# Feed-forward down steps spread over the last pairs, condition rows loaded earlier, and the final norm's first half given precedence

## The chip, the cores and the metric

The kernel runs on one core of one Trainium2 chip. The metric is the device time of one execution in microseconds (us), here the median of three runs. The engines are named as in the profile: PE is TensorE (PEld its weight loads), DVE is VectorE, ACT is ScalarE, POOL is GpSimd, SP is SyncE, whose queue issues most of the loads.

## What is computed

Two layers of a diffusion backbone work on 512 latent tokens and 256 context tokens of 1024 channels. Each layer is a half-step feed-forward, token mixing, and another half-step feed-forward; the output is the final RMSNorm of the latent tokens. Cut to what matters here:

```python
def half_ffn(x, shift, scale, gate, g, w_gate, w_up, w_down):
    h = rmsnorm(x, g) * (1 + scale) + shift
    return x + 0.5 * gate * swiglu(h, w_gate, w_up, w_down)   # silu(h @ w_gate) * (h @ w_up) @ w_down

mod_l = (silu(c) @ ada_w[layer] + ada_b[layer])               # nine shift, scale and gate vectors
...
return rmsnorm(x_l, final_g)
```

The hidden width of the feed-forward is 2816, which is 22 blocks of 128. The four feed-forwards are called f0 and f1 (layer 0) and f2 and f3 (layer 1). f3 computes latent tokens only, since the context isn't needed after it.

## The kernel before, in words

Activations lie with channels on partitions. Every fp32 matrix product is three matmuls on operands split in a rounded high part and a rest (`mm3`, lines 296 to 299): a weight tile of 128x512 is loaded by SP (`wraw`, L132), cast by ACT to its high part (L120) and subtracted by DVE to its low part (L121); that is `wsplit`. There are six raw slots (`w32p`) and eight slots each of high and low parts (`wp`).

A feed-forward (`ffn`) runs over eleven pairs of hidden blocks. The first pair is computed plainly (`Pair`). Each pair j from 1 to 10 builds two matrices (`Mat`), gate and up, each as seven block products of half the tokens (numbers 1 to 7, L478), from sums and differences of weight blocks that POOL forms (L453, L454, L465, L467). A product is twelve matmuls of 384 columns (256 in f3). Between products, ACT copies and DVE combines partial sums (L483, L496), applies the SiLU (L502), multiplies gate and up (L510) and splits the result into the activations `ah` and `al`. The products of one pair are issued as gate 1, the former pair's up 4, gate 5, 2, 6, 3, 7, up 1, gate 4, up 5, 2, 6, 3, 7, so there are 14 to a pair.

The down projection of a finished pair is a generator of eight steps (`dsteps`), one for each block of 128 output channels. A step (`down`, L312) multiplies the two hidden blocks of the pair with their weights into a PSUM tile `sm`, of which there are three, and DVE adds it to the residual stream x with the gate as factor (L323). Before the first and the fifth step, two down weight tiles are loaded and split. When a pair j up to 9 has issued its gate product 5, the eight steps of pair j-1 join a queue, and after every product `dstep` (L533) takes one step from it (two in f0's pair 2). So the steps come between the first eight products after that point, the other six have none, and pair 10 has none. The down projection of the last two pairs (blocks 18 to 21) follows after the loop, first for part of the tokens, then for the others: latent and then context tokens in f0 and f2, two halves of 384 tokens in f1, two halves of 256 latent tokens in f3.

Beside the products, `Background` computes the modulation vectors that later stages need, on DVE. Its condition rows (`scb`, 128x1024) come in two halves: load (L204), Silu on ACT (L205), then for each of its vectors eight steps, each of a 256 KB load (L211) and one or two DVE reductions (L215), which are pinned behind the DVE work traced before them. `tick`, called after each product, takes steps at `rate` per product. There is one slot for the condition rows, so the second half's load waits for the last reduction of the first half. In the neighbourhood mixer the same class loads through POOL's queue. In f3 it has no vectors to compute, and only loads and activates the rows.

`final` (L1102) norms the latent tokens in two halves of 256: squares on ACT, additions on POOL and for the last two on DVE (L254, L255), column sums and a broadcast by matmuls with ones (L259, L274), with twelve small DVE operations between (`st`, L262 to L269) and a scaled diagonal (L272), then eight multiplies on DVE (L1111) into a ring of four tiles, each sent out by SP (L1113).

Order: the program order is a priority. A planner walks the instructions when the kernel is built and puts on each engine the earliest in program order among those that it takes to be ready; a block under `high_priority(offset=400)` counts as 400 instructions earlier. On the chip each engine keeps the order so found.

## Time and profile before

| | us |
|---|---|
| median of three runs | 2666.29 |
| lowest and highest | 2664.46, 2667.95 |
| the profiled execution | 2665.89 |
| its span, first to last instruction | 2664.1 |
| PE busy | 2537.8 (95%) |
| DVE busy | 2127.7 (80%) |
| ACT busy | 1189.4 (45%) |
| POOL busy | 641.6 (24%) |

The mean granted clock of TensorE was 0.979 of its full 2.4 GHz. All times below are microseconds from the start of the profiled span. f0 takes the time to about 595, f1 that from about 950 to 1470, f2 from there to about 1985, f3 from about 2260 to the final norm at 2647. The view of waits tells for each engine whom it waited for; the timeline gives each instruction with its start, its duration and, in brackets, how long its engine stood idle before it and what ended that; the table of stretches gives each engine's busy time in a stretch and the mean granted clock.

### The profile page before, as it was taken

To read this page: it belongs to the slowest core of one execution; us is meant where nothing else is said; L and a number is where in the kernel's file an instruction comes from. 1 tells how busy PE (TensorE), PEld (TensorE's weight loads), DVE (VectorE), ACT (ScalarE), POOL (GpSimd) and SP (SyncE) were. 2 spreads that over 40 slices of the span, in tenths; PEclk is the share of its full clock that TensorE was granted. 3 is DMA by queue.
4 is the path that set the end of the run, shared out by engine and by line. 5 is a ranking of instruction groups with operands and counts; after the bars stand their busy time and mean duration, and the time that the engine had idled before them with its cause. 6 is when DMAs were issued, how large, how long until landed. Compare 5 with 4: busy or idle time off the path is not lost. (4 is left out here: it accounts for less than half of the span.)

```text
span 2664.1 us, 41381 instructions
## 1 busy us (share of the span) xinstructions
PE 2537.8 (95%) x14860; PEld 2321.8 (87%) x14860; DVE 2127.7 (80%) x4316; ACT 1189.4 (45%) x2435; POOL 641.6 (24%) x513
## 2 busy tenths in 40 slices
PE   6999999999999899999999999999999998899997
PEld 4889989987898799999999999999986787899987
DVE  8878888888578687787778879789788775888876
ACT  6533333344238663334334533343335554644443
POOL 2321322221210142132222422222201100433331
PEclk8999999999999899999999999999999999999998
DMA  6334333343465022333332224344432110233332
GB/s 232 96 98 121 102 108 108 104 127 115 147 179 133 15 80 84 107 95 100 99 95 72 83 88 151 119 131 134 124 111 64 49 32 1 83 104 98 97 100 67
DMA packets 145357, 269.92 MB, mean 101 GB/s; under 512 B 17664, under 2 KB 23808, under 8 KB 145152
## 3 DMA queue, kind: packets, MB, share of 16 engines
q1 hardware_dynamic: 139360, 250.82, 30.7%
q0 software_dynamic: 4640, 15.73, 1.8%
q8 instruction: 116, 1.90, 0.3%
q10 hardware_dynamic: 1152, 0.74, 0.1%
q14 instruction: 89, 0.73, 0.1%
HBM read 258.84 MB, written 8.39 MB: 100 GB/s over the span
## 5 line engine op out<-in xcount | busy, mean ns | idle before, releaser
L120 ACT CAST whi<-w 128x512 fp32r<-128x512 f32 (+2 forms) x826 | 500.1, 617 | 777.6 <-PE bg L298 358.2
L121 DVE TENSOR_TENSOR wlo<-w,whi 128x512 fp32r<-128x512 f32 (+2 forms) x826 | 633.5, 785 | 161.7 <-ACT whi L120 153.6
L297 PE MATMUL sm<-ah,whi 128*128 128x512 f32 (+2 forms) x1488 | 512.5, 345 | 11.7 <-DVE x L323 9.8
L298 PE MATMUL sm<-al,whi 128*128 128x512 f32 (+2 forms) x1488 | 511.9, 344 | 0.0
L299 PE MATMUL sm<-ah,wlo 128*128 128x512 f32 (+2 forms) x1488 | 509.8, 343 | 0.0
L323 DVE SCALAR_TENSOR_TENSOR x<-sm,mod,x 128x512 f32<-128x512 f32 (+3 forms) x712 | 421.4, 613 | 56.6 <-PE sm L299 52.3
L297 PEld LDWEIGHTS sm<-ah,whi 128*128 128x128 f32 x1488 | 282.0, 190 | 47.5 <-DVE x L323 15.0
L299 PEld LDWEIGHTS sm<-ah,wlo 128*128 128x128 f32 x1488 | 282.0, 190 | 31.9 <-issue 0.5
L298 PEld LDWEIGHTS sm<-al,whi 128*128 128x128 f32 x1488 | 283.6, 191 | 27.4 <-DVE al L121 0.5
L453 POOL TENSOR_TENSOR s<-w,w 128x512 f32<-128x512 f32 x80 | 106.9, 1337 | 809.7 <-DMA w<-in_ffn_gu 716.4
L467 POOL TENSOR_TENSOR w<-w,w 128x512 f32<-128x512 f32 x80 | 122.4, 1530 | 389.9 <-DVE wlo L121 200.4
L255 POOL TENSOR_TENSOR acc<-acc,sq 128x384 f32<-128x384 f32 (+1 forms) x50 | 46.4, 928 | 427.6 <-ACT sq L254 426.6
L120 ACT CAST whi<-s 128x512 fp32r<-128x512 f32 x80 | 49.7, 621 | 222.1 <-POOL s L453 75.4
L496 DVE TENSOR_TENSOR c<-bg,c 128x384 f32<-128x384 f32 (+1 forms) x160 | 83.4, 521 | 67.0 <-PE bg L299 65.5
L297 PE MATMUL bg<-B11h,whi 128*128 128x384 f32 (+1 forms) x384 | 128.1, 334 | 8.4 <-ACT B11h L120 5.8
L299 PE MATMUL bg<-B11h,wlo 128*128 128x384 f32 (+1 forms) x384 | 128.6, 337 | 5.3 <-DVE wlo L121 5.3
L120 ACT CAST ah<-c 128x384 fp32r<-128x384 f32 (+1 forms) x176 | 85.1, 486 | 103.2 <-DVE c L510 91.4
L298 PE MATMUL bg<-B11l,whi 128*128 128x384 f32 (+1 forms) x384 | 128.2, 334 | 0.0
L465 POOL TENSOR_TENSOR w<-s,w 128x512 f32<-128x512 f32 x80 | 120.1, 1501 | 10.7 <-DVE wlo L121 3.7
L297 PE MATMUL bg<-B22h,whi 128*128 128x384 f32 (+1 forms) x352 | 118.4, 336 | 1.8 <-ACT c L483 1.6
L454 POOL TENSOR_TENSOR w<-w,w 128x512 f32<-128x512 f32 x80 | 116.0, 1449 | 6.3
L297 PE MATMUL bg<-T3h,whi 128*128 128x384 f32 (+1 forms) x320 | 107.5, 336 | 8.6 <-DVE c L496 8.6
(384 smaller groups left out, 6648.0 us busy)
## 6 DMA issues: line engine op xcount, KB each, us to landing
w<-in_ffn_gu SPq DMA_DIRECT2D x352, 256.0 KB, 2.8
gt<-in_ada_t SPq DMA_DIRECT2D x208, 256.0 KB, 2.7
w<-in_ffn_d SPq DMA_DIRECT2D x176, 256.0 KB, 2.9
w<-in_ada_w SPq DMA_DIRECT2D x48, 256.0 KB, 4.6
gt<-in_ada_t POOLq DMA_DIRECT2D x32, 256.0 KB, 3.2
w<-in_ab_in SPq DMA_DIRECT2D x24, 256.0 KB, 2.7
scb<-in_cond_rows SPq DMA_DIRECT2D x8, 512.0 KB, 4.5
w<-in_ab_out SPq DMA_DIRECT2D x16, 256.0 KB, 3.8
```

What stands on the lines that cost most here:

```text
L120: nc.scalar.copy(hi, src)
L121: (eng or nc.vector).tensor_tensor(lo, src, hi.bitcast(F32), op=ALU.subtract)
L255: (nc.vector if i >= len(srcs) - 2 else adder).tensor_tensor(acc[:, :n], acc[:, :n], sq[:, :n], op=ALU.add)
L297: nc.tensor.matmul(out, whi, xhi, start=first, stop=False, skip_group_check=more)
L298: nc.tensor.matmul(out, whi, xlo, start=False, stop=False, skip_group_check=more)
L299: nc.tensor.matmul(out, wlo, xhi, start=False, stop=last, skip_group_check=more)
L323: nc.vector.scalar_tensor_tensor(o, p[:, a - t0:a - t0 + m], gate[:, d, v:v + 1], o, op0=ALU.mult, op1=ALU.add)
L453: nc.gpsimd.tensor_tensor(s1, a21, a22, op=ALU.add)
L454: nc.gpsimd.tensor_tensor(a21, self.src[1], a21, op=ALU.subtract)
L465: nc.gpsimd.tensor_tensor(self.src[6], self.src[5], self.src[6], op=ALU.subtract)
L467: nc.gpsimd.tensor_tensor(self.src[3], self.src[3], self.src[6], op=ALU.subtract)
L496: nc.vector.tensor_tensor(self.c[p], ps, self.c[p], op=ALU.add)
```

## The change

Three things change. `dstep` now adds a fraction to an account after every product and takes a step whenever the account reaches one: 8/14 a product up to pair 8, 8/20 in pairs 9 and 10, two in f0's pair 2 as before. What the queue still holds after the loop is issued there. `Background` yields twice between the load of the second half of the condition rows and its Silu, and twice more before the first reduction that uses it; its rate counts these four. `final` puts all that it does for each half under `high_priority(offset=400)`, adds the squares on DVE instead of POOL, and has eight output tiles.

```diff
-            self.rate = 2 * KD * len(mods) / steps
+            self.rate = (2 * KD * len(mods) + 4) / steps
...
                 self.queue.dma_start(scb, A["cond_rows"][:, :, hs])
+                if half:
+                    yield
+                    yield
                 nc.scalar.activation(scb, scb, AF.Silu)
+                if half:
+                    yield
+                    yield
...
-                    dstep(2 if first and self.j == 2 else 1)
+                    dstep(2.0 if first and self.j == 2 else 8.0 / 14.0 if self.j < np2 - 2 else 8.0 / 20.0)
...
+            paid = [0.0]
+
             def dstep(n):
-                for _ in range(n):
+                paid[0] = min(paid[0] + n, 2.0) if queue else 0.0
+                while paid[0] >= 1.0 - 1e-6:
+                    paid[0] -= 1.0
                     while queue and next(queue[0], 0) == 0:
                         queue.pop(0)
...
                 prev = u
+            while queue:
+                dstep(1.0)
             later.finish()
...
-            fp = pool("fp", 4, st)
+            fp = pool("fp", 8, st)
             for (t0, n, v) in HALVES:
                 sl = slice(t0, t0 + n)
-                pb = rms_rows([xk[k][:, sl] for k in range(KD)], n, D, np_, nc.gpsimd, "sm" if t0 else "nr")
-                for k in range(KD):
-                    o = fp.tile([P, 512], F32, name="o")
-                    nc.vector.scalar_tensor_tensor(o[:, :n], xk[k][:, sl], fg[:, k:k + 1], pb[:, :n],
-                                                   op0=ALU.mult, op1=ALU.mult)
-                    nc.sync.dma_start(A["out"][k][:, sl], o[:, :n])
+                with tc.high_priority(offset=400):
+                    pb = rms_rows([xk[k][:, sl] for k in range(KD)], n, D, np_, None, "sm" if t0 else "nr")
+                    for k in range(KD):
+                        o = fp.tile([P, 512], F32, name="o")
+                        nc.vector.scalar_tensor_tensor(o[:, :n], xk[k][:, sl], fg[:, k:k + 1], pb[:, :n],
+                                                       op0=ALU.mult, op1=ALU.mult)
+                        nc.sync.dma_start(A["out"][k][:, sl], o[:, :n])
```

## Rows read from the trace of the kernel before

**Rows 1.** Busy time, share of the span and instructions of each engine.

```profile
PE 2537.8 (95%) x14860; PEld 2321.8 (87%) x14860; DVE 2127.7 (80%) x4316; ACT 1189.4 (45%) x2435; POOL 641.6 (24%) x513
```

**Rows 2.** Stretches: length, busy us of each engine (instructions), PEclk, DMA share, GB/s.

```profile
482.00:529.00 47.00, 47.00 (x268) 44.10 (x268) 41.12 (x77) 16.97 (x32) 11.23 (x8) 1.00 0.34 107
529.00:561.00 32.00, 29.64 (x166) 28.11 (x165) 29.08 (x56) 13.85 (x27) 7.62 (x5) 1.00 0.44 134
1390.00:1422.00 32.00, 28.24 (x157) 26.58 (x156) 27.54 (x50) 13.21 (x26) 7.39 (x5) 1.00 0.42 129
1918.00:1950.00 32.00, 29.85 (x165) 27.84 (x164) 26.55 (x51) 14.22 (x28) 7.37 (x5) 1.00 0.44 129
2562.00:2592.00 30.00, 30.00 (x205) 27.61 (x206) 22.36 (x38) 14.22 (x30) 11.57 (x8) 1.00 0.34 106
2592.00:2620.00 28.00, 24.30 (x183) 23.23 (x181) 20.33 (x31) 13.41 (x31) 7.23 (x5) 0.94 0.31 95
382.00:389.00 7.00, 6.77 (x23) 6.20 (x24) 5.00 (x10) 1.55 (x3) 0.74 (x1) 0.55 0.22 71
2606.00:2611.00 5.00, 5.00 (x32) 5.00 (x32) 2.77 (x4) 1.48 (x4) 1.29 (x1) 0.66 0.35 92
```

**Rows 3.** Timeline of PE, last pairs: first and last two of nine waits.

```profile
543.74 0.44 PE L297 MATMUL bg<-T2h,whi 128*128 128x384 f32 x1 [1.57 <-ACT c L483]
...
2604.48 0.38 PE L297 MATMUL bg<-B11h,whi 128*128 128x256 f32 x1 [1.60 <-DVE c L510]
2605.71 0.39 PE L297 MATMUL bg<-T2h,whi 128*128 128x256 f32 x1 [0.85 <-ACT c L483]
```

**Rows 4.** Timeline of ACT in f0: the Silu of the second condition rows.

```profile
373.91 1.06 ACT L205 ACTIVATE scb<-scb 128x1024 f32<-128x1024 f32 x1 [2.33 <-DMA scb<-in_cond_rows]
```

**Rows 5.** Timeline of DVE behind it.

```profile
375.01 0.75 DVE L215 CUSTOM_DVE_ANT_0 go<-gt,scb,mod 128x512 bf16<-128x512 f32 x1 [1.70 <-ACT scb L205]
...
375.80 1.66 DVE L215 CUSTOM_DVE_ANT_0 gt<-gt,scb,mod 128x512 f32<-128x512 f32 x1
...
381.43 1.13 DVE L323 SCALAR_TENSOR_TENSOR x<-sm,mod,x 128x512 f32<-128x512 f32 x2
```

**Rows 6.** Timeline of PE behind that.

```profile
382.23 0.79 PE L297 MATMUL sm<-ah,whi 128*128 128x512 f32 x1 [3.16 <-DVE x L323]
```

**Rows 7.** Timeline of DVE in the tail.

```profile
2647.03 0.48 DVE L323 SCALAR_TENSOR_TENSOR x<-sm,mod,x 128x256 f32<-128x256 f32 x1
...
2649.18 0.16 DVE L262 TENSOR_SCALAR st<-sm 128x2 f32<-128x2 f32 x1 [0.43 <-PE sm L259]
...
2651.61 0.16 DVE L269 SCALAR_TENSOR_TENSOR st<-st 128x2 f32<-128x2 f32 x1
2652.38 1.66 DVE L1111 SCALAR_TENSOR_TENSOR o<-x,c_final_g,nr 128x256 f32<-128x256 f32 x4 [0.61 <-PE nr L274]
...
2659.41 1.93 DVE L1111 SCALAR_TENSOR_TENSOR o<-x,c_final_g,sm 128x256 f32<-128x256 f32 x4 [0.42 <-DMA out<-o]
```

**Rows 8.** Timeline of PE in the tail: the first half's broadcast.

```profile
2651.26 1.08 PE L274 MATMUL nr<-dg,ones 128*128 128x256 f32 x2 [2.12 <-DVE st L269]
```

**Rows 9.** Timeline of PE: one down step and the product after it.

```profile
495.37 0.39 PE L297 MATMUL sm<-ah,whi 128*128 128x512 f32 x1
...
496.77 0.28 PE L297 MATMUL sm<-ah,whi 128*128 128x256 f32 x1
...
497.49 0.34 PE L297 MATMUL bg<-T2h,whi 128*128 128x384 f32 x1
```

**Rows 10.** Groups by line, whole span: busy us, mean ns, idle before them.

```profile
L121 DVE TENSOR_TENSOR wlo<-w,whi 128x512 fp32r<-128x512 f32 (+2 forms) x826 | 633.5, 785 | 161.7 <-ACT whi L120 153.6
```

**Rows 11.** Groups by line in the tail, 2628 to the end.

```profile
L255 POOL TENSOR_TENSOR acc<-acc,sq 128x256 f32<-128x256 f32 x10 | 7.4, 736 | 31.1 <-ACT sq L254 30.8
...
L255 DVE TENSOR_TENSOR acc<-acc,sq 128x256 f32<-128x256 f32 x4 | 1.7, 426 | 1.0 <-ACT sq L254 0.6 <-POOL acc L255 0.2
```

**Rows 12.** Waits by engine: who waited for whom, us, times, longest.

```profile
ACT whi L120 <- PE bg L298: 397.1, 264, 5.1
```

## The prediction

> **What bounds the kernel now.** I read the engine totals first: PE is busy 95% of the span, DVE 80%, ACT 45% [rows 1]. So time can only come out where PE waits or runs at half clock, and the next view is the table of stretches [rows 2]. In a steady pair of the first feed-forward (482 to 529) PE is busy all 47.0 us and DVE 41.1 of them; in f3's (2562 to 2592) PE has 30.0 of 30 us. In the last pair of each feed-forward PE is short: 29.6 of 32, 28.2 of 32, 29.9 of 32 and 24.3 of 28 us. There the kernel issues 14 products and no down step, so PE consumes weights fastest just where POOL, ACT and DVE must make them at the same rate as before. The PE timeline names the waits [rows 3]: in the last pairs PE stands idle nine times, 11.5 us in all: 2.36 in f0 (two), 3.46 in f1 (two), 1.97 in f2 (two), 3.71 in f3 (three); the rows show the first and the last two of the nine. Each ends on a combination or copy by DVE or ACT of the product before, which was itself late. After f3's spell the granted clock averages 0.66 over 2606 to 2611 [rows 2], half speed for part of it, which costs another 5 x 0.34 = 1.7 us. Pool of the first edit: 13.2 us.
>
> The second place is in the middle of f0. At 373.91 ACT starts the Silu on the second half of the condition rows after 2.33 us of idling for their DMA [rows 4]; DVE's reduction behind it starts 1.70 us late, and the following one takes 1.66 us instead of 0.75 [rows 5]. The x updates of the down steps come only at 381.43, their PSUM tiles are not freed, and PE idles 3.16 us until 382.23 [rows 6]. Then the granted clock averages 0.55 over 382 to 389 [rows 2], which loses 7 x 0.45 = 3.1 us. Pool: 6.3 us.
>
> The third is the tail. The last x update starts at 2647.03 [rows 7] and the last output multiply ends at 2661.34. Between lies the final norm of both halves: the broadcast matmuls of the first half run only at 2651.26 [rows 8], behind the last down matmul in PE's order, the four-deep output ring makes DVE wait for outgoing DMAs three times (0.42 us at the last, [rows 7]), and the second half's multiplies queue behind the first's.
>
> **Part 1, down steps spread.** Nothing is added or removed. A step is six matmuls of 512 columns and, where context tokens are computed, six of 256: 2.12 us of PE from 495.37 to 497.49, 1.40 of it for the latent tokens alone, which is f3's step [rows 9]. On DVE it is two x updates, 1.13 us for the 512 and the 256 together [rows 5]. Every fourth step issues two weight loads on SP, two ACT casts and two DVE subtractions of 0.79 us mean [rows 10]. Counting the new rates over the 14 products of a pair, steady pairs keep eight steps, now between all products instead of the first eight; pair 9 gets six, and pair 10 four, after product 5 and 6 of gate and 1 and 5 of up. The second weight half of that group thus moves on SP, ACT and DVE past the loads and splits of pair 10's first products. In steady pairs I cost the move at nothing: what hides it is a PE stream without gaps, where the part of a pair without down steps is already full [rows 2]; if that cover goes, see the rival on slots.
>
> In pair 10 four steps give PE 4 x 2.12 = 8.5 us (f3: 5.6) that doesn't need new product weights, and DVE 4 x 1.13 = 4.5 us (f3, taking two thirds: 3.0) plus two subtractions, 1.6 us, that can delay the chain. Net cover is 8.5 - 4.5 - 1.6 = 2.4 us in f0 to f2 and 5.6 - 3.0 - 1.6 = 1.0 in f3; without the subtractions, which needn't lie on the chain, 4.0 and 2.6. Against the idle time above this gives 2.36 + 2.4 + 1.97 + 1.0 = 7.7 us, or 2.36 + 3.46 + 1.97 + 2.6 = 10.4. I take the middle, 9.1; bounds 4.9 (rival 1) and 13.2 (the pool).
>
> The Trainium skill (Perfetto Trace Analysis, Identifying the Most-Contended Engine) says that matmul busy time is a poor measure of headroom, and to use the weight loads' busy share. By that, with 44.1 of 47 us as full [rows 2], the four last pairs lack 2.0, 3.7, 2.3 and (27.6 of 30 as full) 2.5 us, 10.5 together instead of 13.2, and the sum would fall by 2.7 x 9.1/13.2 = 1.9 us. I keep the idle rows, which name their waits.
>
> **Part 2, condition rows.** Per second half: DMA as before, two background steps, Silu, two steps, first reduction. The pace of steps rises by 4/64 to 4/48, so reductions come a little earlier and the total is the same. The DMA keeps its place on SP (POOL in the mixer) behind the last reduction that reads the old rows, so what queues behind it there still waits. What goes is ACT's 2.33 us in front of weight casts and DVE's 1.70 us, and for four steps no reduction asks DVE for time. Next late would be POOL's weight sums that slow DVE from 375.8 on, which happen with every matrix and don't stop PE elsewhere. I take 5.0 of 6.3; low bound 0, if that slowing alone caused the stall. The other nine Silus cost PE nothing now: no spell of PE idling follows them. In f3, whose background has no modulation, the two loads and Silus (1.06 us each, [rows 4]) are issued in the loop instead of at its end; ACT is busy 14.2 of 30 us there [rows 2], so nothing.
>
> **Part 3, final norm.** In the order now, the second half's chain alone would be: first small operation at 2649.18 [rows 7], its twelve operations by 2651.61 at the latest, which is when the last of both chains starts, two diagonal scalings 0.5, broadcast matmuls 1.1 [rows 8], eight multiplies at 0.41 to 0.48 (1.66 and 1.93 for four, in both rows): 2649.2 + 2.4 + 0.5 + 1.1 + 3.5 = 2656.7 against 2661.3, a gain of 4.6. Against it, the first half's column sums and broadcast (0.5 and 1.08 us of PE) now stand inside the last down products, where PE has no gap: 1.6 back. The additions leave POOL (0.736 us) for DVE (0.426) [rows 11]: ten more on DVE, 4.3 us, beside x updates of 0.48 per 0.72 and then 1.44 us of PE time, and the first half's multiplies come on top; DVE is nearly full there, so up to 1.5 us can come back too, or none. I take 3.0, bounds 1.5 and 4.6.
>
> **Sum.** 9.1 + 5.0 + 3.0 = 17.1 us. The profiled execution took 2665.9 us (span 2664.1 and 1.8 around it), 0.4 under the median of the runs: 2666.3 - 17.1 = 2649.2.
>
> **Rivals.** (1) DVE sets the pace of the last pairs. It is busy 29.1, 27.5, 26.6 of 32 and 20.3 of 28 us [rows 2]. If that share is all it can give, adding 6.1 us of DVE work (f3: 4.6) stretches the pairs to 38.7, 39.1, 39.3 and 34.3 us, where PE alone needs 38.1, 36.7, 38.4 and 29.9: 8.3 of 13.2 stays lost, part 1 gives 4.9, the time is 2666.3 - 4.9 - 5.0 - 3.0 = 2653.4. For it: operations of DVE that take twice their time while POOL works, as the 1.66 us [rows 5]. The Trainium skill (SBUF — State Buffer, SBUF: two separate sides) states that of a DVE instruction with two SBUF inputs and a GpSimd instruction that reads SBUF, the one that starts second waits for the whole of the other; by that rule this rival is right. Against it: DVE reached 41.1 of 47 us in the steady pair with POOL at work and PE never waited. Chance 0.18.
> (2) The planner, not the program's order, decides. It issues what is ready, so the four steps may be used as filling in pair 9, where product 1 of the next matrix is used now, and the final's first half may stay behind; parts 1 and 3 fall away, part 2 stays: 2666.3 - 5.0 = 2661.3. Against: the steps' own weights come later in program order now, so they can't be ready as early. Chance 0.13.
> (3) Slower: a down step's split weights occupy two of the eight slots for seven products instead of four. ACT already waits 397 us for PE to release a slot, 264 times [rows 12]. If product weights then come late once per steady pair (27 pairs in the four loops) by 1.57 us, as at 543.74 [rows 3], that is 42 us: 2666.3 - 17.1 + 42 = 2691. It decides from 17.1/27 = 0.63 us per pair upwards. Against: each step's weights are as many as before, and an even use of PE asks for a product weight every 3.3 us instead of 2.1 in the part without down steps. Chance 0.10.
>
> **How the numbers follow.** The forecast has 0.59: 2649, its own range 2642 (the pools, 13.2 + 6.3 + 4.6 = 24.1) to 2657 (4.9, 3.0 and 1.5 for the three parts). The range takes in rival 1 and most of 2, and 3 us below the pools for single PE waits that the loops hold besides the nine: 2639 to 2663. About 0.2%, 5.3 us, is what a measurement of this kernel can tell from no change, so faster means under 2661.0: forecast and rival 1, 0.77; within 0.2%: rival 2, 0.13; slower: rival 3, 0.10.
>
> **What would show it.** Part 1: in the last pairs four groups of down matmuls (sm from ah) between products 5 and the up matrix's 2, PE idle below 4 us over the four, and no drop of the clock at f3's end; rival 1 would show the idle still there under DVE releasers. Part 2: no ACT idle for the condition rows' DMA, and no 3 us PE spell in f0's middle. Part 3: the first half's broadcast before the last down matmul, no DVE wait on outgoing DMAs, and about 10 us from the last x update to the last multiply. Rival 3 would show as PE waiting in steady pairs on whi or wlo. The forecast is wrong if the steady pairs lose what they now have, a PE without gaps.

## The result, and the profile after

The changed kernel took 2705.74 us (median of four runs, 2703.23 to 2707.99) against 2665.38 for the kernel before on the same chip: ratio 1.015, 95% interval 1.0133 to 1.0167. It is 40 us slower, where 17 us less was forecast. (Every ratio below is to the kernel before, run on the same chip.) Its profiled execution has a span of 2702.5 us. The engine totals of its page differ little from before: PE has the same 2538 us of work, DVE 27 us more [rows 1].

```profile
PE 2538.0 (94%) x14860; PEld 2320.3 (86%) x14860; DVE 2154.4 (80%) x4326; ACT 1191.4 (44%) x2435; POOL 641.8 (24%) x503
```

So the time went into waits of PE. To find the stage, I cut each span at the starts of the column-sum matmuls of the norms, which every kernel has in the same places. The rows of PE's timeline below are the cuts at the beginning of f2, of m1 (the second mixer), of f3 and of the tail.

```profile
1474.26 0.80 PE L265 MATMUL sm<-ones,acc 128*128 128x1 f32 x6 [1.72 <-DVE acc L261]
...
2018.56 0.50 PE L265 MATMUL sm<-ones,acc 128*128 128x1 f32 x4
...
2298.23 0.60 PE L265 MATMUL sm<-ones,acc 128*128 128x1 f32 x4 [1.87 <-DVE acc L261]
...
2691.03 0.61 PE L265 MATMUL sm<-ones,acc 128*128 128x1 f32 x4 [1.54 <-DVE acc L261]
```

f2 took 2018.56 - 1474.26 = 544.3 us, f3 2691.03 - 2298.23 = 392.8. The table gives all stages in this way, for every kernel that ran; m0 and m1 are the mixing stages between the feed-forwards. The medians are of all runs of a kernel (two to eleven), the stages of its one profiled execution.

| kernel | median us | f0 | m0 | f1 | f2 | m1 | f3 | tail |
|---|---|---|---|---|---|---|---|---|
| before | 2666.3 | 595.7 | 344.1 | 529.3 | 530.9 | 278.9 | 369.7 | 15.6 |
| after | 2705.7 | 595.3 | 347.1 | 531.9 | 544.3 | 279.7 | 392.8 | 11.5 |
| e1_spread | 2717.2 | 595.7 | 352.3 | 537.9 | 542.7 | 279.2 | 393.6 | 15.7 |
| e2_rest | 2665.7 | 593.3 | 347.5 | 526.2 | 534.3 | 278.0 | 372.9 | 11.5 |
| e3_late | 2667.5 | 594.6 | 348.8 | 527.6 | 531.2 | 276.7 | 370.3 | 11.5 |
| e4_copy | 2699.5 | 600.4 | 349.8 | 532.5 | 547.6 | 276.0 | 380.9 | 11.5 |
| e5_raw | 2708.9 | 597.1 | 348.8 | 532.4 | 544.0 | 279.9 | 393.8 | 11.5 |
| e6_slots | 2692.9 | 597.0 | 349.7 | 532.4 | 545.2 | 278.7 | 376.5 | 11.5 |
| e7_thin | 2677.7 | 597.4 | 346.3 | 532.5 | 544.3 | 275.8 | 361.9 | 11.5 |
| e8_fill | 2698.4 | 598.1 | 350.5 | 532.4 | 546.0 | 277.5 | 383.1 | 11.5 |
| e9_norm | 2662.0 | 591.0 | 345.7 | 528.8 | 530.9 | 276.4 | 371.5 | 11.5 |
| e10_f0rows | 2662.9 | 592.4 | 345.8 | 528.4 | 531.2 | 278.4 | 373.5 | 11.5 |
| e11_few | 2678.7 | 594.0 | 351.6 | 529.0 | 530.7 | 276.3 | 385.0 | 15.7 |
| e12_both | 2677.0 | 597.1 | 350.2 | 532.4 | 543.0 | 277.3 | 363.0 | 11.5 |
| e13_f2fill | 2695.9 | 597.9 | 344.1 | 532.0 | 534.5 | 278.6 | 392.5 | 11.4 |
| e14_f2thin | 2691.3 | 600.1 | 346.3 | 531.6 | 525.8 | 277.3 | 398.6 | 11.5 |

Stages from different executions differ by some us without any cause in the program: e9_norm has before's order of instructions in f0, and its f0 is 4.7 us shorter; e11_few has before's order up to f3, and its m0 is 7.5 us longer. So what stands out for the changed kernel is f3 (+23.1), f2 (+13.4) and the tail (-4.1). In the kernels with the new pace whose edit leaves f2 as it is, f2 takes 542.7 to 547.6 us, and f3, where it is left as it is, 392.5 to 398.6: what an experiment does to f2 or f3 is to be seen against these.

The table of stretches of the changed kernel (columns as in [rows 2]) shows where in a feed-forward it happens: first a steady pair of f0, then the last pairs of f0, f1 and f2, then a steady stretch of f3 and its end.

```profile
480.00:527.00 47.00, 47.00 (x270) 44.77 (x269) 39.68 (x81) 18.24 (x34) 10.29 (x8) 1.00 0.33 107
527.00:560.00 33.00, 31.54 (x180) 29.93 (x179) 30.75 (x61) 12.83 (x25) 7.40 (x5) 1.00 0.44 138
1395.00:1427.00 32.00, 31.29 (x178) 29.72 (x178) 26.11 (x50) 12.58 (x25) 7.11 (x5) 1.00 0.39 116
1936.00:1968.00 32.00, 30.98 (x179) 29.67 (x178) 27.40 (x54) 12.71 (x25) 7.35 (x5) 1.00 0.52 155
2550.00:2587.00 37.00, 33.97 (x232) 30.27 (x231) 29.19 (x43) 16.15 (x35) 13.64 (x9) 1.00 0.29 86
2616.00:2650.00 34.00, 31.99 (x228) 28.92 (x227) 28.43 (x42) 15.41 (x34) 13.93 (x10) 1.00 0.29 86
```

f0's steady pair is as full as it was, and the last pairs lack 1.5, 0.7, 1.0 and 2.0 us where they lacked 2.4, 3.8, 2.1 and 3.7 [rows 2]. But f3's steady stretch, which had no gap, now lacks 3 of 37 us. PE's timeline shows the same gap in each pair: 2.1 us before product 3 of the up matrix (its operand is B22h), for ACT's copy, and half a microsecond before product 7 of the next gate matrix (T3h), for DVE's combination. f3's pairs last 34.3 to 35.7 us where they lasted 31.5 to 31.9.

```profile
2551.03 0.39 PE L303 MATMUL bg<-T3h,whi 128*128 128x256 f32 x1 [0.47 <-DVE c L502]
...
2566.79 0.39 PE L303 MATMUL bg<-B22h,whi 128*128 128x256 f32 x1 [2.10 <-ACT c L489]
```

The wait at 2566.79, followed back. ACT's timeline: the copy that PE waits for (2566.37) stands behind a cast of `ah`, which itself waited 2.19 us for DVE's multiplication.

```profile
2562.37 0.62 ACT L120 CAST whi<-s 128x512 fp32r<-128x512 f32 x1 [1.39 <-POOL s L459]
2563.25 0.62 ACT L120 CAST whi<-w 128x512 fp32r<-128x512 f32 x1 [0.26 <-PE bg L304]
2566.06 0.41 ACT L120 CAST ah<-c 128x256 fp32r<-128x256 f32 x1 [2.19 <-DVE c L516]
2566.37 0.36 ACT L489 COPY c<-bg 128x256 f32<-128x256 f32 x1
```

DVE's timeline: that multiplication takes 1.51 us and the splits ahead of it 1.12 and 1.45, where others of the same shapes take 0.42 and 0.68.

```profile
2561.76 1.12 DVE L121 TENSOR_TENSOR wlo<-w,whi 128x512 fp32r<-128x512 f32 x1
2562.81 0.41 DVE L502 TENSOR_TENSOR c<-sm,c 128x256 f32<-128x256 f32 x1
2563.14 1.45 DVE L121 TENSOR_TENSOR wlo<-s,whi 128x512 fp32r<-128x512 f32 x1
2564.51 1.51 DVE L516 TENSOR_TENSOR c<-c 128x256 f32<-128x256 f32 x1
2565.95 0.68 DVE L121 TENSOR_TENSOR wlo<-w,whi 128x512 fp32r<-128x512 f32 x1
```

POOL's timeline: its three weight sums cover just this time, after it had waited 9.21 us for its raw weights. Each of the three slow operations of DVE starts while a sum runs and ends 0.3 to 0.6 us behind it (2562.33, 2564.04 and 2565.75 are the sums' ends).

```profile
2560.60 1.73 POOL L459 TENSOR_TENSOR s<-w,w 128x512 f32<-128x512 f32 x1 [9.21 <-DMA w<-in_ffn_gu]
2562.41 1.63 POOL L460 TENSOR_TENSOR w<-w,w 128x512 f32<-128x512 f32 x1
2564.12 1.63 POOL L471 TENSOR_TENSOR w<-s,w 128x512 f32<-128x512 f32 x1
```

And the view of waits, over the whole span, has the wait of which [rows 12] shows the value before, 397.1 us: ACT stands 222 us longer before its weight casts until PE frees a slot.

```profile
ACT whi L120 <- PE bg L304: 619.0, 375, 5.1
...
ACT whi L120 <- issue: 70.7, 38, 5.3
```

This growth doesn't say where time is lost. In the kernel before, ACT's idle time before these casts for which the view names no releaser is 169 us more than here:

```profile
ACT whi L120 <- issue: 240.0, 99, 5.3
```

And the wait for PE grows about as much in each of the four feed-forwards (by 64, 51, 49 and 59 us), though f0 and f1 last no longer than before.

Two things are thus candidates in f3: split slots held too long by the down weights, and POOL's sums that now fall on DVE's chain. The profile cannot say which is cause and which is consequence.

### The profile page after: what moved, and what is told of

It is laid out like the page before. It is cut to its first block, busy times and chain, and to the rows that moved or that the text cites. A ratio compares the mean times of both kernels' runs of the same rounds, so it can differ in the third digit from the quotient of the medians.

```text
span 2702.5 us, 41475 instructions
## 1 busy us (share of the span) xinstructions
PE 2538.0 (94%) x14860; PEld 2320.3 (86%) x14860; DVE 2154.4 (80%) x4326; ACT 1191.4 (44%) x2435; POOL 641.8 (24%) x503
## 4 chain that ended last, share of the span: by engine, by line
PE 69%; DVE 17%; issue 5%; ACT 4%; DMA 3%; POOL 1%; SPq 0%; ACTq 0%; DVEq 0%; POOLq 0%
PE bg L303 12%; PE bg L305 11%; PE bg L304 11%; PE sm L304 10%; PE sm L305 10%; PE sm L303 10%; DVE wlo L121 5%; DVE x L329 2%; DMA w<-in_ffn_gu 1%; DVE gt L221 1%; ACT whi L120 1%; DVE c L502 1%; DVE c L516 1%; PE sm L1082 1%; DMA gt<-in_ada_t 1%
## 5 line engine op out<-in xcount | busy, mean ns | idle before, releaser
L121 DVE TENSOR_TENSOR wlo<-w,whi 128x512 fp32r<-128x512 f32 (+2 forms) x826 | 643.3, 791 | 180.4 <-ACT whi L120 177.7
L329 DVE SCALAR_TENSOR_TENSOR x<-sm,mod,x 128x512 f32<-128x512 f32 (+3 forms) x712 | 422.9, 613 | 49.8 <-PE sm L305 46.5
L459 POOL TENSOR_TENSOR s<-w,w 128x512 f32<-128x512 f32 x80 | 113.6, 1421 | 977.9 <-DMA w<-in_ffn_gu 867.0
L305 PEld LDWEIGHTS sm<-ah,wlo 128*128 128x128 f32 x1488 | 282.9, 190 | 29.8 <-issue 0.5
L473 POOL TENSOR_TENSOR w<-w,w 128x512 f32<-128x512 f32 x80 | 108.7, 1358 | 217.1 <-DVE wlo L121 111.2
L471 POOL TENSOR_TENSOR w<-s,w 128x512 f32<-128x512 f32 x80 | 127.8, 1597 | 40.1 <-DVE wlo L121 37.0
L261 POOL TENSOR_TENSOR acc<-acc,sq 128x384 f32<-128x384 f32 (+1 forms) x40 | 40.0, 1000 | 397.1 <-ACT sq L260 396.3
L303 PE MATMUL bg<-T3h,whi 128*128 128x384 f32 (+1 forms) x320 | 110.7, 346 | 24.9 <-DVE c L502 24.7
L460 POOL TENSOR_TENSOR w<-w,w 128x512 f32<-128x512 f32 x80 | 122.1, 1527 | 6.3
L121 DVE TENSOR_TENSOR al<-c,ah 128x384 fp32r<-128x384 f32 (+1 forms) x176 | 92.4, 528 | 30.3 <-ACT ah L120 30.3
```

The costliest lines, as they stand in the source:

```text
L121: (eng or nc.vector).tensor_tensor(lo, src, hi.bitcast(F32), op=ALU.subtract)
L261: (nc.vector if i >= len(srcs) - 2 else adder).tensor_tensor(acc[:, :n], acc[:, :n], sq[:, :n], op=ALU.add)
L303: nc.tensor.matmul(out, whi, xhi, start=first, stop=False, skip_group_check=more)
L305: nc.tensor.matmul(out, wlo, xhi, start=False, stop=last, skip_group_check=more)
L329: nc.vector.scalar_tensor_tensor(o, p[:, a - t0:a - t0 + m], gate[:, d, v:v + 1], o, op0=ALU.mult, op1=ALU.add)
L459: nc.gpsimd.tensor_tensor(s1, a21, a22, op=ALU.add)
```

## The experiments

**Which part.** The first run takes the new pace alone (with the issue of the rest after the loop), the second everything but the pace.

```diff
 e1_spread: before, with
-                    dstep(2 if first and self.j == 2 else 1)
+                    dstep(2.0 if first and self.j == 2 else 8.0 / 14.0 if self.j < np2 - 2 else 8.0 / 20.0)
 e2_rest: after, with
-                    dstep(2.0 if first and self.j == 2 else 8.0 / 14.0 if self.j < np2 - 2 else 8.0 / 20.0)
+                    dstep(2.0 if first and self.j == 2 else 1.0)
```

> The kernel before with the new pace of down steps alone; condition rows and final norm as before. The stage times of the changed kernel put +13 us in f2 and +23 us in f3, where PE now waits in the steady pairs, and -4 us in the tail. If the even pace is the cause (theory P), this kernel takes 2665 + 40 = about 2705 to 2712, with PE waiting about 2 us per up matrix of f3 on ACT's copy of a partial sum. If the Background's new yields and rate are the cause (theory B: f2 has the most of them), it stays within 5 us of 2665.

> The changed kernel with the old pace, one step after each product, so only condition rows and final norm differ from before. Theory P: the steady pairs are as before; f0's stall of 3.2 us idle and 3.1 us of half clock goes, and the tail is 4 us shorter, while the mixer keeps the 3 us that it lost: 2665 - 6 - 4 + 3 = 2658. Theory B: 2695 or more, with f2 and f3 as long as in the changed kernel.

Measured: e1_spread 2717.17 us, ratio 1.0188 (1.0168 to 1.0207); e2_rest 2665.73, ratio 1.0002 (0.9989 to 1.0016). The pace alone costs all of it and more: f1 is 8.6 us longer as well, which it isn't in the changed kernel and which was not followed up (m0's 8.2 us are little more than what executions differ by). The other two parts together, forecast at 8 us, come to nothing that can be measured; 2658 was expected.

**The pace of the last two pairs alone.** In e3_late the pace is one step a product up to pair 8, as before, and 8/20 in pairs 9 and 10; the other parts are in.

```diff
-... else 8.0 / 14.0 if self.j < np2 - 2 else 8.0 / 20.0)
+... else 1.0 if self.j < np2 - 2 else 8.0 / 20.0)
```

> The changed kernel with the old pace up to pair 8 and 8/20 a product in pairs 9 and 10 only. Theory P: steady pairs without PE waits, and the last pairs keep what the spread gave them, up to 11 us over the four: 2648 to 2656, below the kernel with the rest alone. If the spread does in pairs 9 and 10 what it does in steady pairs (waits of 2 us per matrix), it is no better than that kernel, 2658 to 2662.

Measured: 2667.51, ratio 1.0009 (0.9998 to 1.0021). The expectation failed: without the loss in the steady pairs there is still no gain at the end. PE's timeline of f0 shows why. In pair 9, which now has four steps instead of eight, two waits stand where none stood, and pair 10 keeps one, 2.50 us, longer than any of the nine before (the longest of them is 1.74, in f1).

```profile
496.94 0.45 PE L303 MATMUL bg<-B22h,whi 128*128 128x384 f32 x1 [1.28 <-ACT c L489]
...
501.03 0.44 PE L303 MATMUL bg<-T3h,whi 128*128 128x384 f32 x1 [0.80 <-DVE c L502]
...
543.06 0.45 PE L303 MATMUL bg<-B22h,whi 128*128 128x384 f32 x1 [2.50 <-ACT c L489]
```

In f1 it is the same; in f2 and f3 the waits do shrink (2.3 to 1.3 us and 3.7 to 0.7). Over pairs 9 and 10 of the four feed-forwards PE waits 10.2 us, against 12.1 before and 10.5 in e2_rest, which has the other parts and the old pace.

From there on the question is what costs f3 and f2 their 36.5 us.

**ACT's queue.** The wait at 2566.79 ends on a copy that stands behind a late cast. e4_copy gives the copies precedence.

```diff
-                        nc.scalar.copy(self.c[p], out)
+                        with tc.high_priority(offset=60):
+                            nc.scalar.copy(self.c[p], out)
```

> The changed kernel with ACT's copies of partial sums (products 1, 5 and 6) given a precedence of 60 instructions. Theory C (product 3 waits because this copy stands in ACT's queue behind a cast that waits for a DVE multiply): the 2 us waits of f3 and f2 shrink to below 0.7 us and 15 to 30 us come back, 2676 to 2691. Theory S (split weights come late because down weights hold their slots longer): nothing moves, 2701 to 2711.

Measured: 2699.52, ratio 1.0123 (1.0106 to 1.0139). f3 is 11.9 us shorter than in the changed kernel, half of its loss. (f0 and f2 are longer by 5.1 and 3.3, but not by this edit: f2's order of instructions is that of the changed kernel, and e14_f2thin took 600.1 us for f0 in the changed kernel's order.) The time lies between the two expectations. In f3 the waits for ACT's copy are gone and DVE's combinations are waited for instead, as the waits of PE from 2330 to 2560 show (us in total, times, longest):

```profile
PE bg L303 <- DVE c L503: 13.3, 13, 2.6
PE bg L303 <- ACT c L490: 0.5, 2, 0.4
```

So ACT's order accounts for half of f3's loss; the other half reaches PE in another way, so this order isn't the source, or not the only one.

**Raw slots or split slots.** Both are held by the down weights. e5_raw gives f3's down weights two raw slots of their own, e6_slots four split slots (of high and low parts each).

```diff
 e5_raw:
+            rawd = pool("rawd", 2, st) if wi == 3 else None
-   w.append(wsplit(wraw(A["ffn_d"][wi, i][:, t * 512:(t + 1) * 512])))
+   w.append(wsplit(wraw(A["ffn_d"][wi, i][:, t * 512:(t + 1) * 512], rawd)))
 e6_slots:
+            wpd = pool("wpd", 4, st) if wi == 3 else None
-   w.append(wsplit(wraw(A["ffn_d"][wi, i][:, t * 512:(t + 1) * 512])))
+   w.append(wsplit(wraw(A["ffn_d"][wi, i][:, t * 512:(t + 1) * 512]), ring=wpd))
```

> The changed kernel with two raw slots of their own for the down weights of f3, so that they don't take any of the six that the product weights use. f3 lasts 393 us from its second column sums to those of the final norm, against 370 before. Theory R (the down weights' loads, now spread, hold raw slots and so delay the loads from which POOL forms its sums): f3 falls by 10 us or more and POOL's sums start earlier in the matrix, at product 5. Theory S and theory C: f3 stays within 5 us of 393.

> The changed kernel with four slots of their own for the split down weights of f3, so that all eight whi and wlo slots serve products. Theory S (rival 3 of the prediction): product weights are no longer late, f3 falls from 393 to 375 or less. Theory C: the order in which POOL and DVE meet may shift with the plan, but the waits stay: f3 385 or more.

Measured: e5_raw 2708.89, ratio 1.0156 (1.0127 to 1.0186), f3 393.8, with the order of every engine as in the changed kernel: raw slots are not it. e6_slots 2692.88, ratio 1.0096 (1.0067 to 1.0125), f3 376.5 instead of 392.8, its steady pairs 31.8 us. PE's waits from 2330 to 2560 fall from 16.1 and 4.6 us in the changed kernel to 7.7 and 1.8, most of that at the loop's start:

```profile
PE bg L303 <- ACT c L490: 7.7, 9, 3.2
PE bg L303 <- DVE c L503: 1.8, 1, 1.8
```

In the steady pairs, from 2390 on, a wait of 0.21 to 0.49 us is left of the 2.10. The split slots are worth 16.3 us. The planner knows the slots and with more of them puts ACT's and DVE's work in f3 in another order, so this is the worth of the slots together with the order that they allow.

**The converse: the old pace with fewer slots.** e11_few is the kernel before, but in f3 the products split into six slots and the down weights into two of their own, about the shares that the new pace brings about.

```diff
+            wpf = pool("wpf", 6, st) if wi == 3 else None
+            wpd = pool("wpd", 2, st) if wi == 3 else None
-                    self.w[p] = wsplit(self.src[p])
+                    self.w[p] = wsplit(self.src[p], ring=wpf)
-   w.append(wsplit(wraw(A["ffn_d"][wi, i][:, t * 512:(t + 1) * 512])))
+   w.append(wsplit(wraw(A["ffn_d"][wi, i][:, t * 512:(t + 1) * 512]), ring=wpd))
```

> The kernel before, old pace, but in f3 the split product weights have six slots and the down weights two of their own, instead of eight for both. That is the share that the products have in the changed kernel, where a pair of down weights is held through seven products, without its pace. Theory S (slots): products that can be split only six ahead come late, steady pairs of f3 go from 31.5 us to 32.5 to 34.5, f3 from 369.7 to 378 to 390, the time to 2674 to 2687. Rival, slots matter only together with POOL's sums that fall on the splits by the new pace: pairs within 0.5 us of 31.5, 2664 to 2669.

Measured: 2678.74, ratio 1.0041 (1.0014 to 1.0067); f3 385.0 instead of 369.7, its steady pairs 33.0 to 33.3 us, with one wait in each, before product 7 of the gate matrix:

```profile
2529.79 0.39 PE L297 MATMUL bg<-T3h,whi 128*128 128x256 f32 x1 [1.06 <-DVE c L498]
```

15.3 us from the slots alone, at the old pace: the same size as what e6_slots gave back. That fewer slots suffice for such a loss is thus shown; it isn't the same wait (in the changed kernel the long one is before product 3 of the up matrix), and the four runs lie between 2670.6 and 2684.0, with the profiled one the longest.

**POOL's sums beside DVE.** e7_thin is the changed kernel with f3's weight sums on 16 of 512 columns and one clear of the rest; e8_fill has three clears, so that POOL is busy somewhat longer than with the sums (some 7.3 us a matrix instead of 6.1) but, beside the 16 columns, reads nothing from SBUF. Both leave out most of each weight sum in f3, so f3's products are not the full ones.

```diff
+            def wsum(out, x, y, op):
+                if wi != 3:
+                    nc.gpsimd.tensor_tensor(out, x, y, op=op)
+                    return
+                nc.gpsimd.tensor_tensor(out[:, 0:16], x[:, 0:16], y[:, 0:16], op=op)
+                for _ in range(3):                                     # 1 in e7_thin
+                    tc.keep_in_program_order(nc.gpsimd.memset(out[:, 16:512], 0.0))
```

> The changed kernel in which, in f3 alone, POOL's four weight sums of a matrix work on 16 of the 512 columns and clear the rest, so POOL needs some 0.6 us for each instead of 1.3 to 1.7. This leaves out most of the sums. It takes away both the collisions of POOL with DVE and the lateness of the sums: by theories C and R f3 falls to 375 or less, by theory S it stays near 393.

> As the kernel with thin sums, but POOL clears the columns three times, so it is busy as long as with whole sums, some 1.5 us each, only without reading SBUF. This leaves out most of the sums. Theory C (DVE's operations with two SBUF inputs take twice their time, 1.34 against 0.69 us, while POOL reads, and the even pace puts them there): DVE's subtractions are at 0.7 us throughout, the waits on ACT's copy go and f3 is at 378 or less. Theory R (the sums come too late): f3 stays at 388 or more.

Measured: e7_thin 2677.73, ratio 1.0036 (1.0025 to 1.0048), f3 361.9, pairs 31.4; e8_fill 2698.36, ratio 1.0117 (1.0084 to 1.0149), f3 383.1, pairs 33.4. DVE's groups in f3 (2298 to 2600; name, busy us, mean ns, idle before them) show what the clears change. First the changed kernel:

```profile
L329 DVE SCALAR_TENSOR_TENSOR x<-sm,mod,x 128x512 f32<-128x512 f32 x60 | 44.6, 744 | 1.7 <-PE sm L305 0.7
...
L121 DVE TENSOR_TENSOR wlo<-s,whi 128x512 fp32r<-128x512 f32 x17 | 23.7, 1397 | 2.7 <-ACT whi L120 2.7
...
L516 DVE TENSOR_TENSOR c<-c 128x256 f32<-128x256 f32 x22 | 15.8, 719 | 0.5
```

and the same groups of e8_fill (2300 to 2590):

```profile
L329 DVE SCALAR_TENSOR_TENSOR x<-sm,mod,x 128x512 f32<-128x512 f32 x58 | 43.3, 746 | 2.0 <-PE sm L305 1.4
...
L121 DVE TENSOR_TENSOR wlo<-s,whi 128x512 fp32r<-128x512 f32 x16 | 11.4, 711 | 21.1 <-ACT whi L120 21.1
...
L524 DVE TENSOR_TENSOR c<-c 128x256 f32<-128x256 f32 x21 | 8.9, 424 | 0.7
```

The splits of the sums take 711 ns instead of 1397 and the multiplications 424 instead of 719. In the same loop of the kernel before (2280 to 2560) they took 1164 and 511:

```profile
L121 DVE TENSOR_TENSOR wlo<-s,whi 128x512 fp32r<-128x512 f32 x17 | 19.8, 1164 | 2.3 <-ACT whi L120 1.5
...
L510 DVE TENSOR_TENSOR c<-c 128x256 f32<-128x256 f32 x22 | 11.2, 511 | 0.5
```

DVE's slowing is thus gone, yet PE still waits 0.80 us for ACT's copy in each matrix: the sums beside DVE are worth 9.7 us, and a lateness remains. By the time alone e8_fill can't be told from the changed kernel, since the intervals of the ratios overlap; the 383.1 us lie outside the 392.5 to 398.6 of f3 left as it is, and between the two expectations. e7_thin shows that the lateness goes as well when POOL is merely done sooner: 21.2 us between the two runs, at the same slots (20.6 by their medians). My reading is that with few slots POOL's sums stand in a chain from a slot's release to the next product, with nothing split ahead; that is argued from these runs and not shown step by step.

The even pace didn't bring DVE's slowing, though. Take DVE's operations on two SBUF tiles in the six pairs from product 7 of pair 2's up matrix to that of pair 8's, and add up what the slow ones take beyond the shortest of their kind: in f3 that is 20.1 us before and 21.2 in the changed kernel. In e6_slots it is 24.7 with pairs of 31.8 us, in e11_few 14.1 with pairs of 33.1. So in f3 the slowing was there all along, and with all eight slots for products it cost PE next to nothing; what the pace took away is the cover. f2 has 15.3 before and 18.9 after, f1, which lost nothing, 13.9 and 17.0.

**Both.** e12_both has e6_slots' slots and e8_fill's sums (and leaves out the same part of f3's sums).

> The changed kernel with four slots of its own for f3's split down weights and with f3's weight sums on 16 of 512 columns, the rest of POOL's time filled with clears that read nothing; it leaves out most of each sum in f3, so f3's products are not the full ones. Theory A, slots and POOL's reads are two costs that add: f3 392.8 - 16.3 - 9.7 = 366.8, steady pairs at 31.4 or less, time 2680 +-4. Rival, both remove the same lateness: f3 374 to 377 as with the slots alone, 2689 to 2693.

Measured: 2676.95, ratio 1.0052 (1.0033 to 1.007); f3 363.0, 29.8 us less than in the changed kernel, pairs 31.3 to 31.4. PE's waits from 2330 to 2560:

```profile
PE bg L303 <- ACT c L498: 1.8, 1, 1.8
PE bg L303 <- DVE c L511: 0.5, 1, 0.5
```

Over the stage the two add, with 3.8 us more than their sum (16.3 + 9.7 = 26.0): with the slots, POOL may take as long as it did (e7_thin's 361.9 is hardly shorter). In the steady pairs themselves the slots bring 2.5 us a pair (34.3 to 31.8), the reads 0.9 (to 33.4) and both 3.0 (to 31.3), somewhat less than the sum; the rest lies at the loop's start, where it takes 36.6 us from product 7 of the first gate matrix to that of the second in the changed kernel, 39.9 with the slots, 34.7 without the reads and 31.7 with both. So they are two costs, of which the slots are the larger in a steady pair. f3 is shorter here than in the kernel before, but that kernel's POOL sums are whole, so this says nothing of the pace being better; the kernel before without POOL's reads was not run.

**f2.** The same two runs as for the sums, but for f2 (they leave out most of f2's weight sums instead of f3's).

```diff
-                if wi != 3:
+                if wi != 2:
```

> The changed kernel with f2's weight sums on 16 of 512 columns and the rest of POOL's time filled with clears that read nothing; f2's products are not the full ones, since most of each sum is left out. f2 took 544.3 us against 530.9 before. Theory C (POOL's reads slow DVE's splits and reductions, as 1.24 and 1.79 us ahead of the wait at 1627.19): the waits of 1.0 to 2.9 us before product 3 go, pairs 46.1 to 46.8, f2 530 to 535, time 2692 to 2697. Theory S (slots: ACT's casts wait for PE, DVE idles and then has its work all at once): waits stay at 1 us or more in half the pairs, f2 538 to 544, time 2700 to 2706.

> The same with one clear instead of three, so that POOL is also done sooner and the raw slots come free earlier; f2's sums are left out as in the run above. Theory C: no shorter than with three clears, within 2 us. Theory S or lateness of the raw weights: f2 another 3 us shorter or more than with three clears, to 528 to 538.

Measured: e13_f2fill 2695.85, ratio 1.0113 (1.008 to 1.0145), f2 534.5 instead of 544.3; e14_f2thin 2691.32, ratio 1.0096 (1.0066 to 1.0125), f2 525.8. PE's waits from 1540 to 1930, the changed kernel first:

```profile
PE bg L303 <- DVE c L502: 10.7, 7, 2.9
```

and e13_f2fill:

```profile
PE bg L303 <- DVE c L510: 0.9, 2, 0.6
```

In f2's steady pairs it is POOL's reading that makes DVE late: seven waits become two, and from product 7 of the first pair's up matrix to that of the last the loop is 15.6 us shorter (407.7 instead of 423.3), of which f2's beginning, 5.8 us longer in this execution, takes back a part. With one clear the pairs are as long as with three (46 to 47.2 in both), so an earlier end of POOL's work brings nothing there; the further 8.7 us of e14_f2thin, which as a sum are what the other expectation said, lie at f2's beginning, where e13_f2fill has two waits of 3.9 us and e14_f2thin one of 2.1. With the reads gone f2's pairs are no longer than before (46.1 to 47.7); whether more slots would have done the same was not tried.

**The other two parts.** e9_norm is the kernel before with part 3 alone; e10_f0rows adds part 2 in f0 alone.

```diff
 e10_f0rows, beside part 3:
-            self.rate = 2 * KD * len(mods) / steps
+            self.late = late
+            self.rate = (2 * KD * len(mods) + (4 if late else 0)) / steps
...
+                if half and self.late:
+                    yield
+                    yield
                 nc.scalar.activation(scb, scb, AF.Silu)
+                if half and self.late:
+                    yield
+                    yield
...
-            later = Background(mods, 14.0 * (np2 - 2), None if first else gs)
+            later = Background(mods, 14.0 * (np2 - 2), None if first else gs, late=first)
```

> The kernel before with part 3 (the final norm) alone. On every engine the instructions ahead of the tail keep the order they had. Theory T, part 3 is worth what its stage shows (15.6 to 11.5 us) and nothing else moves: 2666.3 - 4.1 = 2662.2, all stages up to the last column sums as before within 1 us. Rival, the addition of squares and the first half's norm inside the last down steps cost the end of f3 what the tail gains: 2666.

> The kernel before with part 3, and part 2 in f0 alone; pace of the down steps, mixer and the other feed-forwards as in the kernel before. Theory T, part 2 gives f0's stall back (the pair of 52.8 us becomes 46.6) and only a changed plan in the stages behind takes it away: f0 between 589 and 594 against 595.7, and if the stages behind keep their lengths 2662.2 - 2 to 6 = 2656 to 2660. Rival, any change of f0's order moves single waits in the stages behind by some us each, as with parts 2 and 3 together: 2662 to 2668, f0 shorter but m0 or f2 longer.

Measured: e9_norm 2661.96 (11 runs, 2657.43 to 2667.22) against 2664.53 for the kernel before on that chip, ratio 0.9995 (0.9986 to 1.0005); e10_f0rows 2662.89, ratio 0.999 (0.9981 to 1.0). By its medians part 3 brings 2.6 us, about what was expected of it, but the interval doesn't separate this from nothing. PE's timeline of e9_norm has the first half's broadcast ahead of the second half's column sums by 8 us:

```profile
2636.22 0.67 PE L274 MATMUL nr<-dg,ones 128*128 128x256 f32 x2
2644.19 0.61 PE L259 MATMUL sm<-ones,acc 128*128 128x1 f32 x4 [1.54 <-DVE acc L255]
```

Part 2 adds nothing to it: f0 takes 592.4 us with it and 591.0 without. The pair with the condition rows is shorter (46.7 instead of 49.5), but the pairs around it are longer (43.1, 47.7 and 47.7 instead of 42.3, 46.6 and 46.7). Behind it m0 and f2 keep their lengths (345.8 and 531.2 us), so it is not a changed plan further back that takes the gain away. No kernel that ran is measurably faster than the one before.

## Why the prediction was wrong

**Part 1, steady pairs, costed at nothing: this is the step that failed.** It cost f3 23.1 and f2 13.4 us. The cover named for the move, a PE without gaps, said that PE had no slack. It said nothing of the slack of what feeds PE, and that was spent: the part of a pair without down steps was the time in which all eight split slots held product weights. With even steps two of the eight are always a down step's. My rival 3 had this mechanism, its place and the row to look at [rows 12], at a chance of 0.10, and its 2691 us lies nearer to the result than the forecast does. Its sign, PE waiting on whi or wlo, didn't show: in the steady pairs PE waits for ACT's copies and DVE's combinations, which the late splits push back. It was mis-sized as well: it put 1.57 us on all 27 pairs, and that 42 us is near to the 36.5 of f2 and f3 is luck. Measured, f0 and f1 lost nothing that stands out (-0.4 and +2.6), while f3 lost some 3 us a pair. My argument against it, that an even pace asks for product weights less often, fits f0 and f1, and not f3, whose products are of 256 columns instead of 384: a pair needs as many tiles in 31.5 us as elsewhere in 46.5. That this ratio is why f3 is hit hardest is argued; that slots, with the order that they allow, are worth 15 to 16 us there is shown from both sides (e6_slots, e11_few), and so is that POOL's time is part of it (e7_thin, e8_fill).

The Trainium skill (Perfetto Trace Analysis, Optimization Strategy) says that the same gap repeating on the engine that should be busy can mean that there isn't room enough for the next tile. The gap of 2.1 us in every steady pair of f3, and its fall to 0.21 with four more slots, agree.

**Rival 1's mechanism was real, in another place.** I looked for DVE beside POOL in the last pairs, and there it didn't decide. In the steady pairs it does: without POOL's reads f2 is 9.8 us shorter (of 13.4 lost) and f3 9.7 (of 23.1). What I held against it, that DVE reached 41.1 of 47 us without a wait of PE [rows 2], was true, but only as long as enough was split ahead: in f3 DVE lost as much time beside POOL before (20.1 us in six pairs) as after (21.2). The Trainium skill (SBUF — State Buffer, SBUF: two separate sides) names the pairing, a DVE instruction with two SBUF inputs and a GpSimd instruction that reads SBUF; e8_fill and the untouched x updates, one of whose inputs is in PSUM, agree with it.

**Part 1, last pairs, -9.1.** In the profile it looks right: PE lacks 5.2 us in the four stretches, where it lacked 12.0 [rows 2] and I expected under 4, and the clock stays at 1.00 to f3's end. But e3_late shows that this was no gain. The four steps that pair 10 gets are taken from pair 9, which is left with four of its eight there (in the changed kernel with six, two of them pair 8's; nothing is left to issue after the loop), and the waits appear in pair 9; the changed kernel too has one of 2.33 us in f1's. The step that failed is "net cover": I counted what the steps bring to pair 10 and not what they leave where they came from. From product 7 of pair 8's up matrix to the next column sums, the four feed-forwards of e3_late take 432.2 us together, against 434.7 before and 433.4 in e2_rest: 1 to 2 us instead of 9.1. The clock's part of the pool, 1.7 us, isn't even there in e2_rest, where the clock stays at 1.00 over 2590 to 2625 with the waits as before. Two slips in the working changed nothing: one of the nine waits (2604.48) ends on the multiplication of gate and up and not on a combination or copy, and the 2.5 us that f3 lacks by its weight loads are 2.8 when worked out as the other three.

**Part 2, -5.0.** Half of what I expected to see came: the 3.16 us spell of PE is gone in the changed kernel. But ACT still idles for the rows' DMA, now 3.28 us (ACT's timeline); the planner puts the Silu some ten instructions earlier in ACT's order than it did. A wait of PE of 1.51 us stands behind it (PE's timeline), for what I had named as next late: POOL's sums, which run from 357.79, and beside which two splits of DVE's take 1.24 and 1.78 us (DVE's timeline, the last fence):

```profile
356.42 1.06 ACT L208 ACTIVATE scb<-scb 128x1024 f32<-128x1024 f32 x1 [3.28 <-DMA scb<-in_cond_rows]
```

```profile
363.24 0.44 PE L303 MATMUL bg<-T3h,whi 128*128 128x384 f32 x1 [1.51 <-DVE c L502]
```

```profile
359.77 1.24 DVE L121 TENSOR_TENSOR wlo<-s,whi 128x512 fp32r<-128x512 f32 x1 [0.53 <-ACT whi L120]
360.94 1.78 DVE L121 TENSOR_TENSOR wlo<-w,whi 128x512 fp32r<-128x512 f32 x1
```

The pool was mis-sized too. 3.1 of its 6.3 us were the half clock after the spell [rows 2]. e9_norm, with the same order of instructions, idles 2.64 us in that place, until 379.75, and the clock afterwards is full; its table of stretches:

```profile
379.00:386.00 7.00, 6.25 (x35) 5.73 (x36) 6.66 (x13) 2.56 (x5) 1.52 (x1) 1.00 0.27 92
```

In e11_few, in the same order again, PE idles 2.86 us until 381.43 and the clock averages 0.62 over 380 to 384. So the pool is some 2.6 to 4.6 us in other executions, and in e10_f0rows the pairs around it are longer by as much as the pair with the rows is shorter.

**Part 3, -3.0.** Right in its steps. The tail went from 15.6 to 11.5 us in every kernel with it, 4.1 against the 4.6 worked out; the rows of the changed kernel's tail show the broadcast inside the down steps (PE) and the eight multiplications in one run without waits for outgoing DMAs (DVE), where [rows 7] had them.

```profile
2683.08 0.67 PE L280 MATMUL nr<-dg,ones 128*128 128x256 f32 x2
```

```profile
2695.84 3.22 DVE L1124 SCALAR_TENSOR_TENSOR o<-x,c_final_g,sm 128x256 f32<-128x256 f32 x8 [1.32 <-PE sm L280]
```

The 1.6 us that the early matmuls were to take back fit e9_norm's f3, which is 1.8 longer, though single stages vary by more, so that this fit may be luck.

**Sum.** In the two profiled executions f3 +23.1, f2 +13.4, the other four stages together +6.0 and the tail -4.1 make +38.4 us of span (2664.1 to 2702.5). Against f3's and f2's loss stand what slots (16.3) and POOL's reads (9.7 and 9.8) are worth. In f3 that is more than was lost, since the reads slowed DVE in the kernel before as well. The 6.0 us of f0, m0, f1 and m1 are no more than such stages vary, and are left unexplained; why f2 and not f0, which has the same columns and a background too, is hit by POOL's reads stays open.

## What to carry to other kernels

An engine without gaps shows that it is fed, not that its feeders have slack: before spreading work evenly, count for how long each buffer will be held, and look for the wait of the producer on free buffers, which here was in the profile of before. It is a reason to try and no forecast: the same wait grew as much in f0 and f1, which lost nothing. A slowing that is covered in the profile of before belongs into the count too, as it shows as soon as the cover goes. Work put into a stage with gaps is taken from another stage, and its absence there belongs into the sum. And a stall's price in one execution, the clock behind it above all, needs a second execution before it becomes a pool.

## What the runs showed of the hardware

DVE's subtraction of two SBUF tiles (128x512) beside POOL's sums takes about twice its time in the mean, 1397 ns against 711 beside POOL's clears; the x updates, with one input from PSUM, take 744 and 746. It is thus what POOL reads, not that it works, that slows DVE. The single instructions show how. Of the 153 weight splits of DVE in f3 of the changed kernel (2298 to 2600), 50 take more than 0.95 us. Each of the 50 starts while an operation of POOL's runs, 49 of them under a weight sum, and each ends 0.55 us after that operation does. Of the other 103, at 0.7 us, 101 start under no operation of POOL's and two under one of another kind (L373). So here a subtraction that starts under a weight sum is through only after it, and doesn't merely run slower.

With the same instructions in the same order, PE's granted clock averaged 0.55 over 382 to 389 after an idle spell of 3.16 us in one execution, 0.62 over 380 to 384 after one of 2.86 us in another, and 1.00 over 379 to 386 around one of 2.64 us in a third.
